# Three 1024 x 1024 x 1024 products of a hybrid encoder layer by Strassen's scheme, with weight operands made ahead and kept in DRAM

## The chip, the cores and the metric

The kernel runs on one core of one Trainium2 chip. The metric is the device time of one execution in microseconds (us); the times are the median and the extent of three runs. One further execution was taken by the hardware profiler, and all rows come from it.

## What is computed

One layer of a streaming encoder for 1024 tokens of width 1024, in f32. The change touches three products, `o @ W_attn_o`, `(gelu(gate) * hr) @ W_lru_o` and `mixed @ W_out`, each 1024 x 1024 by 1024 x 1024:

```python
h = rms_norm(x, norm_mix)
lru_in, lru_gate, q, k, v, g_lru, g_attn = split(h @ w_in)
hr = rg_lru(causal_depthwise_conv(lru_in, conv_w, conv_b), ...)
y_lru = (gelu(lru_gate) * hr) @ w_lru_o
y_attn = diff_attention(q, k, v, ...) @ w_attn_o
mixed = sigmoid(g_lru) * y_lru + sigmoid(g_attn) * y_attn
x = x + mixed @ w_out
x = x + memory_cross_attention(x, mem, ...)
x = x + hierarchical_moe(rms_norm(x, norm_ffn), ...)
```

## The kernel before

Every product is made of three matmuls per tile (`mm3`, L158): an f32 operand is split into a high part `h` (rounded to the engine's f32r by an ACT copy) and the remainder `l` (a DVE subtraction), and `wh*xh + wl*xh + wh*xl` is accumulated in PSUM. A matmul takes 128 x 128 stationary and 128 x 512 moving elements, so a 1024-cubed product has 8 x 2 x 8 x 3 = 384 of them.

All large tiles live in one pool `S` of 51 slots of 128 x 1024 f32. PSUM has four single banks (`bank`, 512 columns) and two double banks (`bank2`, 1024 columns). Weights come through the class `Weights`: a list of pieces of 512 KB in order of use, each loaded raw by SP's DMA queue (L78), copied to `wh` by ACT (L97) and subtracted to `wl` by DVE (L101). `W.tick` runs that stream ahead of the matmuls by up to `split_ahead` pieces; `W.take` hands over the next ones. The loads are tied to matmuls that went before. SP's queue has at most eight DMAs in flight, each waiting for the one eight places before it. Within an engine the instructions run in the order that the framework's scheduler gave them; the program's text, the waits and the slots that come free decide that order.

The stages, with their times in the trace: norm and start (0 to 40 us); q/k/v (to 304), where `tm_proj` (L331) makes 48 matmuls into a double bank for a quarter of a unit, ACT copies the bank out twice (`sq` L350 and `tm` L351), DVE and POOL apply norm and rotation, PE transposes (`pT`), ACT copies to `qk` (L375) and SP stores it to DRAM (L379); attention with the gate projections (to 711); the LRU, whose last chunks overlap the memory keys and values (to 910); then the three products. The attention output (L859 to L867, `pya`, 910 to 998) and the LRU output (L879 to L892, `pyr`, to 1085) loop over 8 blocks of output channels with the weight stationary (`cm_unit`); DVE multiplies the gate in and adds. w_out (L1209 to L1222, `pwo`, to 1175) has the mixed activation stationary, and adds x. After it the tokens are normalised (`st_A`), transposed (`phc`) and enter the cross attention (`pcq`, to 1358); 32 experts end the program (to 1946).

The lines that the prediction's steps touch:

```python
for j in range(2):                                  # tm_proj, L334
    for k in range(8):
        mm3(ps[:, j, :], hH[k][:, c], hL[k][:, c], wh, wl, k == 0, k == 7)
    W.tick(1)
...
def cm_unit(w, xh, xl, ps_halves):                  # 48 matmuls for a block of 128 output channels
```

Of the kernel before, what the change touches and what calls it, by code (L numbers as in the profile page):

```python
# [131 lines left out]
def block_kernel(ctx, tc, a):  # L132
# [198 lines left out]
    def tm_proj(w, qr, name):  # L331

        ps = bank2(name, F32, (P, 2, 512))
        for j in range(2):  # L334
            c = slice((2 * qr + j) * P, (2 * qr + j) * P + P)
            for k in range(8):
                wh, wl = (x[:, (k % 2) * 512:(k % 2) * 512 + 512] for x in w[k // 2])
                mm3(ps[:, j, :], hH[k][:, c], hL[k][:, c], wh, wl, k == 0, k == 7)
            W.tick(1)
        return ps  # L340

# [58 lines left out]

    W.split_ahead = 4
# [296 lines left out]
    zr, lru = [], {}  # L698
# [43 lines left out]
    def lru_scan(c):  # L742
# [23 lines left out]
        V.scalar_tensor_tensor(zr[c], zr[c], 0.5, q, op0=OP.mult, op1=OP.mult)  # L766
# [38 lines left out]
    def memory_values():  # L805
        w = W.take(4)
        vh, vl = slot("mvH", F32R, (P, 2, 512)), slot("mvL", F32R, (P, 2, 512))
# [11 lines left out]
    OS = 2  # L819
    oH, oL, oraw = [], [], []  # L820

    def o_split():
        for h in range(NH):
            oraw.append(slot(f"or{h}"))
            nc.sync.dma_start(oraw[h], oT_d[h])
            oH.append(slot(f"oH{h}", F32R))
            oL.append(slot(f"oL{h}", F32R))
            if OS == 1:
                split(oraw[h], oH[h], oL[h])
                oraw[h] = None  # L830
        for c in (slice(0, 512), slice(512, 1024)):
            for h in range(NH):
                if OS == 2:
                    split(oraw[h][:, c], oH[h][:, c], oL[h][:, c])
        oraw.clear()
# [4 lines left out]
    for op in LSEQ:  # L840
# [4 lines left out]
        elif op == "mv":  # L845
            mvH, mvL = memory_values()
        elif op == "mt":
            mkH, mkL = memory_keys_T(ktm)
        elif op == "o":
            o_split()  # L850
# [7 lines left out]
    ma = []  # L858
# [9 lines left out]
    del oH, oL  # L868


    zH, zL = [], []
    for c in range(8):
        zH.append(slot(f"zH{c}", F32R))
        zL.append(slot(f"zL{c}", F32R))
        split(zr[c], zH[c], zL[c])
    del zr
    mH, mL = [], []
    for j in range(8):
        w = W.take()[0]  # L879
        tr, m = slot(f"trb{j}"), ma[j]  # L880
        nc.sync.dma_start(tr, tg_d[8 + j])
        ps = bank2(f"pyr{j}")
        cm_unit(w, zH, zL, [ps[:, 0:512], ps[:, 512:]])
        V.scalar_tensor_tensor(tr, tr, 1.0, ps, op0=OP.add, op1=OP.mult)
        V.tensor_tensor(m, m, tr, op=OP.add)
        mH.append(slot(f"mH{j}", F32R))
        mL.append(slot(f"mL{j}", F32R))
        A.activation(mH[j], m, AF.Copy, scale=0.5)
        V.scalar_tensor_tensor(mL[j], m, 0.5, f(mH[j]), op0=OP.mult, op1=OP.subtract)
        W.tick()  # L890
        ma[j] = None
    del zH, zL, m  # L892
# [310 lines left out]
    x1 = []  # L1203
    for tb in range(NB):
        t = slot(f"x1_{tb}")
        nc.sync.dma_start(t, a["x"][tb * P:(tb + 1) * P, :])
        x1.append(t)
# [314 lines left out]
```

## Time and profile before

| | us |
|---|---|
| median of three runs | 1949.65 |
| lowest, highest | 1947.31, 1950.56 |
| the profiled execution | 1948.1 |
| its span in the trace | 1946.3 |
| PE busy | 1868.9 |
| DVE, ACT, POOL busy | 1296.6, 1103.5, 327.8 |
| attention output, LRU output, w_out | 88, 87, 90 |

The span is that of the core's instructions; the time around it is 1.8 us. A busy share of an engine is an average over stages of different kinds. What a stage can win is read in its own stretch of the trace, from the engine that is never idle there and from the waits that end last.

### The profile page before, as it was taken

What the parts mean: (1) busy time and instruction counts of PE and PEld (TensorE: products, weight loads), DVE (VectorE), ACT (ScalarE), POOL (GpSimd) and SP (SyncE); (2) the same over time, 40 slices, a digit from 0 to 9 for tenths busy, and PEclk for the clock granted to TensorE, in tenths of its full rate; (3) what the DMA queues carried; (4) which work ended last, traced back from release to release, by engine and by line L of the source; (5) the groups of instructions that cost most, each with busy time, mean ns of one, the idle gap of its engine ahead of it and who ended that gap; (6) DMA issues with size and microseconds to landing.
All of it is one profiled execution on the core that took longest, in us unless ns stands there. A gap on an engine that the chain in (4) does not pass through costs nothing. (4 is left out here: it accounts for less than half of the span.)

```text
span 1946.3 us, 25814 instructions
## 1 busy us (share of the span) xinstructions
PE 1868.9 (96%) x9214; PEld 1491.7 (77%) x9214; DVE 1296.6 (67%) x1766; ACT 1103.5 (57%) x1631; POOL 327.8 (17%) x432
## 2 busy tenths in 40 slices
PE   6999999999999999899999999996999999999996
PEld 5888888888888888778888887875777777777664
DVE  5222324677777758887444425675899999999985
ACT  5233324555555546876212215452888888888885
POOL 2144430122222221100000001111111111111110
PEclk9999999999999999999999999997999999999998
DMA  5222244433333121225322401177999999999996
GB/s 201 86 87 87 87 134 137 125 108 107 111 118 120 55 101 57 71 90 187 108 77 86 187 22 65 56 281 272 322 355 346 337 349 358 353 348 338 348 367 218
DMA packets 115027, 353.40 MB, mean 182 GB/s; under 512 B 14864, under 2 KB 28304, under 8 KB 114896
## 3 DMA queue, kind: packets, MB, share of 16 engines
q1 hardware_dynamic: 102992, 322.11, 46.9%
q0 software_dynamic: 7296, 17.04, 3.8%
q10 hardware_dynamic: 4608, 12.58, 1.6%
q8 instruction: 73, 1.20, 0.2%
q14 instruction: 58, 0.48, 0.1%
HBM read 311.82 MB, written 48.23 MB: 185 GB/s over the span
## 5 line engine op out<-in xcount | busy, mean ns | idle before, releaser
L101 DVE TENSOR_TENSOR wl<-wraw,wh 128x1024 fp32r<-128x1024 f32 x480 | 576.9, 1227 | 123.7 <-ACT wh L97 111.7
L97 ACT ACTIVATE wh<-wraw 128x1024 fp32r<-128x1024 f32 x480 | 496.3, 1057 | 113.0 <-PE pgu L161 15.9
L160 PE MATMUL pgu<-wl,xeh 128*96 128x512 f32 x512 | 203.7, 398 | 1.0 <-DVE wl L101 1.0
L159 PE MATMUL pgu<-wh,xeh 128*96 128x512 f32 x512 | 203.7, 398 | 0.3 <-ACT wh L97 0.3
L161 PE MATMUL pgu<-wh,xel 128*96 128x512 f32 x512 | 201.2, 393 | 0.0
L505 ACT ACTIVATE p<-pS,st 128x256 f32<-128x256 f32 (+7 forms) x128 | 94.9, 747 | 103.3 <-DVE st L498 51.7
L159 PE MATMUL pga<-hH,wh 128*128 128x512 f32 x320 | 127.4, 398 | 2.5 <-DVE wT L539 2.5
L160 PE MATMUL pga<-hL,wh 128*128 128x512 f32 x320 | 126.0, 394 | 0.0
L161 PE MATMUL pga<-hH,wl 128*128 128x512 f32 x320 | 125.5, 392 | 0.0
L160 PEld LDWEIGHTS pgu<-wl,xeh 128*96 128x96 f32 x512 | 82.9, 162 | 43.5 <-DVE wl L101 12.5
L159 PEld LDWEIGHTS pgu<-wh,xeh 128*96 128x96 f32 x512 | 83.0, 162 | 33.8 <-ACT wh L97 0.5
L161 PEld LDWEIGHTS pgu<-wh,xel 128*96 128x96 f32 x512 | 82.9, 162 | 33.4 <-DVE xel L329 0.2
L1351 POOL DMA_INDIRECT out<-y,idx x32 | 46.4, 1451 | 357.8 <-ACT y L1350 352.9
L514 POOL TENSOR_SCALAR p<-p,st 128x128 f32<-128x128 f32 (+3 forms) x64 | 55.0, 860 | 305.2 <-DVE st L513 159.4
L160 PE MATMUL py<-wl,ah 128*96 128x512 f32 x256 | 101.7, 397 | 0.3 <-DVE wl L101 0.2
L161 PE MATMUL py<-wh,ah 128*96 128x512 f32 x256 | 100.4, 392 | 0.0
L159 PE MATMUL pqk<-wh,hH 128*128 128x512 f32 x256 | 100.3, 392 | 0.0
L161 PE MATMUL pqk<-wh,hL 128*128 128x512 f32 x256 | 100.2, 391 | 0.0
L160 PE MATMUL pqk<-wl,hH 128*128 128x512 f32 x256 | 99.7, 389 | 0.0
L375 ACT ACTIVATE qk<-pT,gq 128x512 f32<-128x512 f32 x32 | 20.2, 686 | 106.8 <-PE pT L374 93.9
L159 PE MATMUL py<-wh,ah 128*96 128x512 f32 x256 | 80.0, 393 | 0.3 <-ACT wh L97 0.3
L493 PE MATMUL pS<-kH,qS 128*128 128x512 f32 (+2 forms) x192 | 69.5, 365 | 5.2 <-ACT p L505 5.2
(527 smaller groups left out, 4415.8 us busy)
## 6 DMA issues: line engine op xcount, KB each, us to landing
wraw<-in_w_gu SPq DMA_DIRECT2D x256, 512.0 KB
wraw<-in_w_dn SPq DMA_DIRECT2D x128, 512.0 KB
wraw<-in_w_cm SPq DMA_DIRECT2D x32, 512.0 KB
x<-in_x SPq DMA_DIRECT2D x16, 512.0 KB
wraw<-in_w_qk SPq DMA_DIRECT2D x32, 256.0 KB
qk_d<-qk SPq DMA_DIRECT2D x32, 256.0 KB
qr<-qk_d SPq DMA_DIRECT2D x32, 256.0 KB
kr<-qk_d SPq DMA_DIRECT2D x32, 256.0 KB
```

The lines of the kernel that those rows point to most:

```text
L97: ins = nc.scalar.activation(h, raw, AF.Copy)
L101: nc.vector.tensor_sub(l, raw, h.bitcast(F32))
L159: W.seen(E.matmul(out, lh, rh, start=start, stop=False))
L160: E.matmul(out, lh, rl, start=False, stop=False)
L161: E.matmul(out, ll, rh, start=False, stop=stop)
L375: A.activation(out[i][:, :, c], pt, AF.Copy, scale=gq[:, i:i + 1])
L493: E.matmul(ps[:, o:o + c], lhs, kh_[h, m][:, o:o + c], start=True, stop=False)
L505: A.activation(p[:, :n], ps[:, :n], AF.Exp, bias=mx[:, m:m + 1], accum_out=ls[:, m:m + 1])
L514: G.tensor_scalar(pp[1][:, :n], pp[1][:, :n], rl[:, 1:2], 0.0, op0=OP.mult, op1=OP.add)
L1351: G.indirect_dma_start(out=a["out"][:, :], out_offset=bass.IndirectOffsetOnAxis(ap=dest, axis=0), in_=y, in_offset=None, bounds_check=T - ...
```

## The change

Each of the three products is computed with seven products of half size (512 x 512 x 512, Winograd's form of Strassen's scheme): `multiply` runs, for each of the seven, four blocks of 128 output rows with four steps of 128 along the sum and `mm3`, 7 x 4 x 4 x 3 = 336 matmuls in place of 384. Seven operands on each side are sums of the four quarters of a matrix (`operand_steps`).

For the weights they are made during q/k/v: `prepare` loads the 24 quarters (512 KB each), forms the sums on DVE, splits each of the 42 operand tiles into `ph` and `pl` and stores both to DRAM (`pre_d`, 84 stores of 512 KB). `tm_proj` takes two steps of it at every tick (`PRE`). In the product they are loaded again (`preloaded`, 84 loads). For the activations `computed` makes them while the product before runs. Output sums run on DVE between the half-size products (`u1` to `u3`), and the gates are multiplied in by quarters (`gated`, `x1_add`). The 24 weight pieces leave the stream. The LRU's last step writes its result as quarters (`zq`), and o is loaded as quarters.

```diff
-    pieces += [a["w_ao"][j] for j in range(8)]
-    pieces += [a["w_lo"][j] for j in range(8)]
-    for hf in range(2):
-        pieces += [a["w_out"][hf, j] for j in range(4)]
...
             W.tick(1)
+            for _ in range(PRE[0]):
+                next(pre, None)
...
+    def operand_steps(q, moving, emit):
+        def lin(to, x, y, op):
+            for t, u, v in zip(q[to], q[x], q[y]):
+                V.tensor_tensor(t, u, v, op=op)
+        ADD, SUB = OP.add, OP.subtract
+        yield emit(0, q[0])
+        yield emit(1, q[2 if moving else 1])
+        for args in (((1, 3, 1, SUB), (0, 1, 0, ADD), (2, 2, 0, SUB)) if moving else
+                     ((2, 2, 3, ADD), (0, 2, 0, SUB), (1, 1, 0, SUB))):
+            yield lin(*args)
+        yield emit(2, q[0])
+        yield lin(0, 3, 0, SUB)
+        for n, i in ((3, 1), (4, 2), (5, 0), (6, 3)) if moving else ((3, 0), (4, 3), (5, 2), (6, 1)):
+            emit(n, q.pop(i))
+            yield
...
+            def emit(p, tiles):
+                h, l = slot(f"ph{n}{lp}{p}", F32R), slot(f"pl{n}{lp}{p}", F32R)
+                split(tiles[0], h, l)
+                nc.sync.dma_start(pre_d[n][p, lp, 0], f(h))
+                nc.sync.dma_start(pre_d[n][p, lp, 1], f(l))
+                if p == 5 and u + 1 < len(units):
+                    nxt.append(load(*units[u + 1]))
...
+    PRE[0] = 2
     for kind, i in order[1:len(order) - NL]:
         run(qk_steps(i) if kind == "qk" else v_steps(i))
+    run(pre)
...
+    def multiply(n, before, out):
+        lane = stages[n][2]
+        p1, u2, u3 = [None] * 2, [None] * 2, [None] * 2
+        for p in range(7):
+            g = 7 * n + p
+            ta, tb_ = ops.pop((g, 0)), ops.pop((g, 1))
+            for blk in range(4):
...
+                for k in range(4):
+                    rh, rl = (x[:, (k % 2) * 512:(k % 2) * 512 + 512] for x in tb_[k // 2])
+                    mm3(ps, *lane(ta, blk, k), rh, rl, k == 0, k == 3)
+                if blk == 0:
+                    if p < 6:
+                        before(p + 1)
+                    for d, kind in ((1, "computed"), (2, "preloaded")):
+                        for side in range(2):
+                            if (g + d) // 7 < len(stages) and stages[(g + d) // 7][side].__name__ == kind:
+                                operands(g + d, side)
...
+                if p == 0:
+                    A.activation(p1[lp][:, c], ps, AF.Copy)
+                elif p in (2, 3):
+                    to, x = (u2, p1) if p == 2 else (u3, u2)
+                    V.tensor_tensor(to[lp][:, c], x[lp][:, c], ps, op=OP.add)
+                else:
+                    out(p, blk, ps, {1: p1, 4: u3, 5: u3, 6: u2}[p][lp], c)
+                if p == 5:
+                    V.tensor_tensor(u2[lp][:, c], u2[lp][:, c], ps, op=OP.add)
...
-    for j in range(8):
-        w = W.take()[0]
-        t = slot(f"tga{j}")
-        nc.sync.dma_start(t, tg_d[j])
-        ps = bank2(f"pya{j}")
-        cm_unit(w, oH, oL, [ps[:, 0:512], ps[:, 512:]])
-        W.tick()
-        V.scalar_tensor_tensor(t, t, 1.0, ps, op0=OP.add, op1=OP.mult)
-        ma.append(t)
...
+    stages.append((preloaded("w_lo"), computed(zq, True), lane_out))
+    multiply(0, *gated(0, False))
+    stages.append((computed(mq, False, 0.5), preloaded("w_out"), lane_sum))
+    multiply(1, *gated(8, True))
...
+        if p == 5 and blk == 3:
+            W.split_ahead = 4
+            st_A(0)
+        if p == 6 and blk == 1:
+            st_A(1)
...
+    multiply(2, x1_load, x1_add)
```

Three places show how the order of the work changes. The first is SP's queue in q/k/v, from the stores of the second unit's first half (`qk_0`) to those of its second half (`qk_2`). Before, two weight pieces of 512 KB stood between them:

```order
L379 DMA qk_d_321<-qk_0_0_1067 128x512
L379 DMA qk_d_322<-qk_0_0_1067 128x512
L379 DMA qk_d_321<-qk_0_1_1068 128x512
L379 DMA qk_d_322<-qk_0_1_1068 128x512
L78 DMA wraw_1362<-in_w_qk 128x2x256 x2
L78 DMA wraw_1393<-in_w_qk 128x2x256 x2
L379 DMA qk_d_321<-qk_2_0_1239 128x512
```

In the changed kernel (its first twelve rows of 25; `phw_lo` and `plw_lo` are high and low part of an operand, `qw_lo` a quarter):

```order
L379 DMA qk_d_321<-qk_0_0_1160 128x512
L379 DMA qk_d_322<-qk_0_0_1160 128x512
L379 DMA qk_d_321<-qk_0_1_1161 128x512
L379 DMA qk_d_322<-qk_0_1_1161 128x512
L454 DMA pre_w_lo<-phw_lo_1412 128x1024
L455 DMA pre_w_lo<-plw_lo_1413 128x1024
L454 DMA pre_w_lo<-phw_lo_1443 128x1024
L454 DMA pre_w_lo<-phw_lo_1449 128x1024
L455 DMA pre_w_lo<-plw_lo_1444 128x1024
L455 DMA pre_w_lo<-plw_lo_1450 128x1024
L78 DMA wraw_1515<-in_w_qk 128x2x256 x2
L454 DMA pre_w_lo<-phw_lo_1518 128x1024
```

Between the two groups of `qk_d` stores now stand 14 operand stores, four quarter loads and the same two weight pieces.

The second is ACT in the same unit, from the copies of the first transposes (`qk_0`) to the copy of the second product out of PSUM (`sq_1`, `tm_1`). Before:

```order
L375 ACTIVATE qk_0_0_1067<-pT_0_0_1069,gq 128x2x256
L375 ACTIVATE qk_0_1_1068<-pT_0_1_1075,gq 128x2x256
L97 ACTIVATE wh_1106<-wraw_1018 128x1024
L97 ACTIVATE wh_1137<-wraw_1049 128x1024
L350 ACTIVATE sq_1_1145<-pqk_1_1081 128x1024
L351 ACTIVATE tm_1_1144<-pqk_1_1081 128x1024
```

In the changed kernel:

```order
L375 ACTIVATE qk_0_0_1160<-pT_0_0_1162,gq 128x2x256
L375 ACTIVATE qk_0_1_1161<-pT_0_1_1168,gq 128x2x256
L97 ACTIVATE wh_1199<-wraw_1097 128x1024
L324 ACTIVATE phw_ao_1206<-qw_ao_937 128x1024
L324 ACTIVATE phw_ao_1212<-qw_ao_935 128x1024
L97 ACTIVATE wh_1250<-wraw_1135 128x1024
L324 ACTIVATE phw_ao_1257<-qw_ao_933 128x1024
L324 ACTIVATE phw_lo_1263<-qw_lo_1218 128x1024
L350 ACTIVATE sq_1_1270<-pqk_1_1174 128x1024
L351 ACTIVATE tm_1_1269<-pqk_1_1174 128x1024
```

Four operand copies (`phw`) were put in between the weight copies and the two copies out of PSUM. In the fourth unit the same four stand there, in the first and the third unit one.

The third is DVE where the attention output begins: `op1` is an operand computed from the quarters of o (`oq`), `zq`, `r`, `i` and `q` belong to the last two LRU chunks. In the changed kernel:

```order
L921 TENSOR_TENSOR op100l<-oq_8148,op100h 128x1024
L921 TENSOR_TENSOR op101l<-oq_8150,op101h 128x1024
L411 TENSOR_TENSOR oq_8152<-oq_8160,oq_8152 128x1024
L826 SCALAR_TENSOR_TENSOR i_8189<-i_8189,xc_7979 128x1024
L836 SCALAR_TENSOR_TENSOR zq_8218<-gl_7821,q_8013 128x512
L836 SCALAR_TENSOR_TENSOR zq_8220<-gl_7821,q_8013 128x512
L411 TENSOR_TENSOR oq_8148<-oq_8152,oq_8148 128x1024
L411 TENSOR_TENSOR oq_8154<-oq_8162,oq_8154 128x1024
L824 SCALAR_TENSOR_TENSOR r_8188<-q_8211,r_8188 128x1024
L874 SCALAR_TENSOR_TENSOR mkL<-pmkT_8226,vec,mkH 128x512
L874 SCALAR_TENSOR_TENSOR mkL<-pmkT_8233,vec,mkH 128x512
L411 TENSOR_TENSOR oq_8150<-oq_8154,oq_8150 128x1024
```

Before, 16 subtractions `oL<-or,oH` of 512 columns stood here together, ahead of the last chunk's steps; now the operands' subtractions and sums alternate with them.

## Rows read from the trace of the kernel before

**Rows 1.** The page's head and part 1: busy time and share of each engine.

```profile
span 1946.3 us, 25814 instructions
...
PE 1868.9 (96%) x9214; PEld 1491.7 (77%) x9214; DVE 1296.6 (67%) x1766; ACT 1103.5 (57%) x1631; POOL 327.8 (17%) x432
```

**Rows 2.** Stretches (columns in the first line), the three rewritten stages.

```profile
core 0: us, PE busy (x) PEld busy (x) DVE busy (x) ACT busy (x) POOL busy (x), PEclk, DMA share, GB/s
...
910.00:998.00 88.00, 87.69 (x392) 72.33 (x391) 45.15 (x47) 32.79 (x41) 0.00 (x0) 1.00 0.31 103
998.00:1085.00 87.00, 87.00 (x385) 72.07 (x384) 34.88 (x29) 14.06 (x14) 0.61 (x4) 1.00 0.33 113
1085.00:1176.00 91.00, 90.84 (x413) 75.17 (x412) 33.14 (x40) 17.23 (x24) 2.97 (x8) 1.00 0.25 96
```

**Rows 3.** Waits of PE from 900 to 1190 us: total, times, longest.

```profile
PE pcqT L953 <- ACT cq L940: 0.7, 1, 0.7
PE pcq L159 <- DVE phc_0s L329: 0.3, 1, 0.3
PE pya L160 <- DVE oL L329: 0.3, 1, 0.3
PE pwo L159 <- DVE phc_0s L329: 0.2, 1, 0.2
```

**Rows 4.** Timeline of PE in w_out: start, duration.

```profile
1159.65 0.39 PE L160 MATMUL pwo<-wl,mH 128*128 128x512 f32 x1
1159.87 0.39 PE L161 MATMUL pwo<-wh,mL 128*128 128x512 f32 x1
...
1160.78 0.39 PE L159 MATMUL pwo<-wh,mH 128*128 128x512 f32 x1
```

**Rows 5.** Groups by line, 909 to 1176 us: busy us, mean ns, idle before.

```profile
L101 DVE TENSOR_TENSOR wl<-wraw,wh 128x1024 fp32r<-128x1024 f32 x25 | 30.3, 1219 | 1.8 <-ACT wh L97 1.2 <-PE pwo L160 0.5
L97 ACT ACTIVATE wh<-wraw 128x1024 fp32r<-128x1024 f32 x24 | 24.9, 1051 | 49.3 <-PE pwo L160 14.5 <-PE pya L161 10.5 <-DVE wl L101 10.4
...
L1217 DVE TENSOR_TENSOR x<-x,pwo 128x512 f32<-128x512 f32 x16 | 11.0, 687 | 46.5 <-PE pwo L161 46.5
```

**Rows 6.** Stretches: q/k/v, its stores, loads alone, experts (columns as Rows 2).

```profile
72.00:304.00 232.00, 232.00 (x1090) 193.46 (x1089) 66.91 (x55) 76.54 (x95) 92.59 (x96) 1.00 0.30 98
122.00:124.00 2.00, 2.00 (x11) 1.65 (x10) 0.31 (x1) 2.00 (x4) 0.00 (x0) 1.00 1.06 408
900.00:905.00 5.00, 5.00 (x24) 4.14 (x23) 5.00 (x5) 1.06 (x1) 0.00 (x0) 1.00 1.03 419
...
1392.00:1800.00 408.00, 408.00 (x1937) 288.00 (x1936) 374.95 (x380) 350.23 (x416) 56.78 (x46) 1.00 0.99 347
```

**Rows 7.** Timeline of the end of w_out.

```profile
1175.07 1.91 PE L920 MATMUL phc<-ident,tn 128*128 128x128 f32 x16
1177.29 0.50 PE L159 MATMUL pcq<-wh,phc_0s 128*128 128x512 f32 x1 [0.32 <-DVE phc_0s L329]
```

**Rows 8.** Timeline of SP in q/k/v: start, issue time of the group.

```profile
121.04 1.83 SPq L379 DMA_DIRECT2D qk_d<-qk  x4
...
138.22 1.82 SPq L379 DMA_DIRECT2D qk_d<-qk  x4
...
163.84 1.82 SPq L379 DMA_DIRECT2D qk_d<-qk  x4
...
186.97 1.82 SPq L379 DMA_DIRECT2D qk_d<-qk  x4
...
232.52 1.82 SPq L379 DMA_DIRECT2D qk_d<-qk  x4
...
258.14 1.80 SPq L379 DMA_DIRECT2D qk_d<-qk  x4
```

**Rows 9.** Timeline of ACT, second q/k unit.

```profile
148.73 1.03 ACT L351 ACTIVATE tm<-pqk 128x1024 f32<-128x1024 f32 x1
153.44 1.03 ACT L350 ACTIVATE sq<-pqk 128x1024 f32<-128x1024 f32 x1 [3.68 <-issue]
```

**Rows 10.** Groups by line, 72 to 304 us.

```profile
L97 ACT ACTIVATE wh<-wraw 128x1024 fp32r<-128x1024 f32 x18 | 18.1, 1069 | 0.0
```

More of the change, by code (lines that the diff above doesn't have):

```diff
@@ L765, in lru_scan @@
         yield
-        V.scalar_tensor_tensor(zr[c], zr[c], 0.5, q, op0=OP.mult, op1=OP.mult)
+        for hf in range(2):
+            i = 2 * (c // 4) + hf
+            if c % 2 == 0:
+                zq.setdefault(i, []).append(slot(f"zq{i}{c // 2 % 2}"))
+            tc_ = slice(TH[hf], TH[hf] + 512)
+            V.scalar_tensor_tensor(zq[i][-1][:, (c % 2) * 512:(c % 2) * 512 + 512], zr[c][:, tc_], 0.5, q[:, tc_],
+                                   op0=OP.mult, op1=OP.mult)
+        zr[c] = None
         yield
@@ L817, in memory_values, with half_T @@
         return vh, vl
[L819 to L835, printed above, removed]
+    def half_T(name, src, i, lp):
+        return quarter(name, src[4 * (i // 2) + 2 * lp:4 * (i // 2) + 2 * lp + 2, :, TH[i % 2]:TH[i % 2] + 512]
+                       .rearrange("h p c -> p h c"))
@@ new lines, in block_kernel, with preloaded @@
+    stages, ops = [], {}
+    QUARTER = {1: 0, 4: 2, 5: 3, 6: 1}
+    def preloaded(name):
+        while True:
+            for p in range(7):
+                r = []
+                for lp in range(2):
+                    t = [slot(f"{name}{p}{lp}{x}", F32R) for x in "hl"]
+                    for i in range(2):
+                        d = nc.sync.dma_start(f(t[i]), pre_d[name][p, lp, i])
+                        W.after(d, W.last)
+                    r.append(t)
+                yield r
@@ new lines, in computed, with emit @@
+    def computed(q, moving, scale=None):
+        done = []
+        def emit(p, tiles):
+            r = []
+            for lp, t in enumerate(tiles):
+                h, l = slot(f"op{len(ops)}{p}{lp}h", F32R), slot(f"op{len(ops)}{p}{lp}l", F32R)
+                if scale is None:
+                    W.after(A.activation(h, t, AF.Copy), W.last)
+                    V.tensor_tensor(l, t, f(h), op=OP.subtract)
+                else:
+                    W.after(A.activation(h, t, AF.Copy, scale=scale), W.last)
+                    V.scalar_tensor_tensor(l, t, scale, f(h), op0=OP.mult, op1=OP.subtract)
+                r.append((h, l))
+            done.append(r)
+        steps = operand_steps(q, moving, emit)
+        for _ in range(7):
+            while not done:
+                next(steps)
+            yield done.pop()
@@ L849, in block_kernel @@
         elif op == "o":
-            o_split()
+            oq = {i: [half_T(f"oq{i}{lp}", oT_d, i, lp) for lp in range(2)] for i in range(4)}
+            stages.append((preloaded("w_ao"), computed(oq, True), lane_out))
+            operands(0, 0)
+            operands(0, 1)
+            operands(1, 0)
         elif op == "s2":
@@ L876, in block_kernel @@
[L876 to L891, printed above, removed]
@@ L892, in block_kernel, with gated, before, out @@
-    del zH, zL, m
+    mq = {i: [None, None] for i in range(4)}
+    def gated(j0, add):
+        tg, tmp = {}, {}
+        def before(p):
+            if p in QUARTER:
+                i = QUARTER[p]
+                tg[i] = [half_T(f"tg{j0}_{i}{lp}", tg_d[j0:j0 + 8], i, lp) for lp in range(2)]
+        def out(p, blk, ps, prev, c):
+            i, lp = QUARTER[p], blk // 2
+            t = tg[i][lp]
+            if p in (1, 4) and lp not in tmp:
+                tmp[lp] = slot(f"y{j0}_{p}{lp}")
+            y = tmp[lp] if p in (1, 4) else prev
+            V.tensor_tensor(y[:, c], prev[:, c], ps, op=OP.add)
+            if blk % 2 == 1:
+                V.scalar_tensor_tensor(t, t, 1.0, y, op0=OP.add, op1=OP.mult)
+                m = mq[(0, 2, 1, 3)[i]]
+                if add:
+                    V.tensor_tensor(m[lp], m[lp], t, op=OP.add)
+                else:
+                    m[lp] = t
+                tg[i][lp] = None
+                tmp.pop(lp, None)
+        return before, out
```

100 lines of the change are left out of this document (73 added, 27 removed).

## The prediction, made before the change was run

> **What bounds the kernel now.** I read the page's first part first: TensorE is busy for 1868.9 of the 1946.3 us of the span, so a matmul taken away shortens the program unless something else takes its place [rows 1]. Then the table by stretches: in the three stages that the change rewrites (910 to 998, 998 to 1085, 1085 to 1176 us) PE is busy 87.69, 87.00 and 90.84 us of 88, 87 and 91 at a granted clock of 1.00, the higher of the two levels (2.4 GHz), while DVE is busy 33 to 45 us, ACT 14 to 33 and the DMA engines a quarter to a third [rows 2]. The list of waits says the same: from 900 to 1190 us PE waits 1.5 us in all [rows 3]. These stages are made of matmuls and nothing else. The reader should take one price from the timeline, the distance between two starts: 1159.65, 1159.87, ... 1160.78, five steps in 1.13 us, so 0.2265 us each [rows 4]. (The 0.39 us of a row is a modelled duration that overlaps the next one.) A check: 384 x 0.2265 = 87.0 us, the length of a stage.
>
> **What is removed.** Each 1024 x 1024 x 1024 product falls from 384 matmuls to 7 x 4 x 4 x 3 = 336 of the same form. 3 x 48 = 144 x 0.2265 = **-32.6 us**, all of it on the path.
>
> **What is added beside these matmuls.** Of the 24 weight pieces the splits go (24 ACT copies of 1.05 us, 24 DVE subtractions of 1.22 us) [rows 5]. In come, per product, 14 operand copies on ACT, 14 subtractions and 8 sums on DVE, and the output sums. With 1.22 us for 1024 columns and 0.69 for 512 [rows 5] DVE has about 54, 65 and 56 us of work in stages of 336 x 0.2265 = 76 us. It fits, and a half-size product (48 matmuls, 10.9 us) lies between the filling of a bank and its next use, so output sums have 10.9 us where they need up to 6. I cost them at nothing. If that cover is gone at a boundary, PE waits for the bank, a rival below. The reloads bring 44.0 MB in place of 12.6 MB. The stages now move some 103, 113 and 96 GB/s [rows 2], about 27.7 MB; 31.4 MB more in 233 us is 254 GB/s, against 419 GB/s in a stretch of nothing but loads [rows 6]. Nothing there either.
>
> **At two seams I count a loss.** The attention output starts with computed operands: eight quarter loads of o and four operand loads (6.3 MB, 15.4 us at the rate of the writes below) go out when the last readers of hH leave, then the subtractions and sums stand between the last scan's steps on DVE (the order above). By hand op110l ends about 1 us after PE wants it and op120l 0.3 us after: +1.5 us, bounds 0 and 6 (a late o quarter). At the end, the last two x blocks are complete only after the last half-size product, and the normalisation, the transposes and the first pcq follow at once. Before, pcq began 2.2 us after the transposes [rows 7]; by hand I get 3 us of idle PE against about 1: +2 us, bounds 0 and 4.
>
> **Where I see the real cost: q/k/v.** Here the change adds work to a stage in which PE is busy for 232.00 of 232 us, and adds DMA above all: 84 stores of 512 KB (44.0 MB) and 24 quarter loads (12.6 MB) on SP's one queue, beside 98 GB/s x 232 us = 22.7 MB at a busy share of 0.30 [rows 6]. A stretch that is mostly such stores ran at 408 GB/s with the engines full [rows 6], so the additions are 56.6 / 0.408 = 139 us of full DMA; with the 70 us already there, 209 of 232. Two steps per tick finish the 67 steps in 34 of 40 ticks, so the last 36 us get less and the earlier part is fuller still. I therefore count between the q/k stores, whose issue times stand in SP's timeline [rows 8]. SP keeps its order, so what stands between two of them must fit there:
> - 121.04 to 138.22 us: 8 stores, with the q/k and weight traffic 6.3 MB, 15.4 us in 17.2
> - 138.22 to 163.84: 10 stores and 4 quarters, 9.4 MB, 23.1 in 25.6
> - 163.84 to 186.97 (the order above): 14 stores and 4 quarters, 11.5 MB, **28.3 in 23.1**
> - 186.97 to 232.52: 16 stores and 4 quarters, 14.7 MB, 36.0 in 45.5
> - 232.52 to 258.14: 12 stores and 4 quarters, 10.5 MB, 25.7 in 25.6
>
> The third is over by 5.2 us. Who waits when DMA is late? Not only SP: the slots of the stored operands are reused, so ACT's copies of pqk out of PSUM wait until certain stores have landed, and PE has two double banks. In the second unit the copy of pqk1_1 ended at 148.73 + 1.03 = 149.76; the copy of the next product could start at 153.44, so PE took the freed bank at about 153.2: 3.4 us of slack [rows 9]. In the changed order four more ACT copies of 1.07 us [rows 10] stand ahead of it, 4.3 us, and its wait for the landing of two stores (2.6 us at 408 GB/s) comes on top: 1 to 3.5 us of idle PE, again in the fourth unit; in the first and the third only one copy is added, and they keep their slack. 5.2 + 2 x 2.3 = **+10 us**, bounds 0 (all of it slips into gaps) and 21 (the rate of the experts, rival 2). I take 10 because the rows nearest to stores, those of the q/k stores, ran at 408. The added ACT and DVE time itself (42 copies, 45 us; 42 subtractions and 24 sums, 81 us) fits beside the 76.54 and 66.91 us of the 232 there [rows 6].
>
> **Behind it.** Attention and LRU keep their work; 24 pieces fewer pass through the weight stream there. In the experts DMA is at 0.99 with 347 GB/s while PE is busy throughout [rows 6]; their loads are tied to PE's progress, so the stage starts earlier with its loads and keeps its length: nothing. If the loads were the limit there, they too would start earlier.
>
> **Sum**, on the profiled execution (1948.1 us): 1948.1 - 32.6 + 10 + 1.5 + 2 = 1929.0. The median shown is 1.55 us higher, so **1930.5 us** in its terms, its own range 1924 to 1938.
>
> **A rule against the change.** By this trace the engines carry 408 to 419 GB/s for short stretches and 347 at a share of 0.99 for 408 us [rows 6]. The Trainium skill, page "DMA: Bandwidth & Descriptors", section Specifications, gives a limit of about 358 GB/s of HBM per core. By that figure, as an estimate, the five windows would be over by some 14 us in place of 5.2, and the sum would be 1939. The short stretches speak against it as a hard limit; the 408 us are near it.
>
> **Rivals.**
> 1. *No stall in q/k/v.* Landings come before the copies need them. For it: between the groups of [rows 8] SP's queue holds only four weight loads each, so there is room to slip into. Then 1949.65 - 32.6 + 3.5 = **1920.5**. Chance 0.20.
> 2. *The sustained rate holds*: 347 / 0.99 = 350 GB/s, as in the experts. The five windows would then need 18.0, 26.9, 32.9, 42.0 and 30.0 us; four are over, by 0.8 + 1.3 + 9.8 + 4.4 = 16.3 us in place of 5.2. So 11 more is lost: **1941.5**. For it: 408 us of trace at that rate. Against it: that stretch has scattered transfers too, this one none. Chance 0.17.
> 3. *The queue locks PE to DMA* (the other side). A weight load for the next unit stands in SP's queue behind stores that wait for ACT; ACT waits to copy pqk until earlier stores have landed; PE waits for ACT. If every round of copy, store (eight in flight, 8 x 0.524 / 0.408 = 10.3 us), landing and copy costs more than a product and its transposes (12 us), each of the 16 products grows. It is slower from 29.1 / 16 = 1.8 us per product on; at 3 us, 48 us are lost: 1930.5 - 10 + 48 = **1968**. For it: the waits are in the order, and a full window leaves nothing to catch up with. Against it: most stores are waited for more than a product later. Chance 0.17.
> 4. *Product boundaries stall.* 21 boundaries of which each waits 1 us for operands or banks: 1930.5 + 21 = **1951**. For it: DVE is at 70 to 85% of these stages with PE in lockstep. Against it: 10.9 us of cover. Chance 0.09.
> The forecast keeps 0.37.
>
> **How the numbers follow.** 0.2% is 3.9 us, about what a measurement of this kernel can tell. Rivals 1 and 2 and the forecast are faster, 0.74 together; rival 4 is about the same, 0.09; rival 3 is slower, 0.17; with a little of the forecast's tail that is 0.73, 0.09 and 0.18. The range runs from below rival 1 (its two seams also at nothing: 1917, and 1 for the runs' spread) to 1955, beyond rival 4: left out is rival 3 with its long tail, and little else.
>
> **What would show it.** Right: 336 matmuls per stage and stages of 76 to 79 us; q/k/v 5 to 15 us longer, with PE's waits naming ACT's copies of pqk (their banks) or w_qk splits, and DMA near full between 121 and 260. Wrong: q/k/v unchanged (rival 1); PE waiting 40 us or more there (rival 3); PE waiting for DVE sums or for operands in the three stages (rival 4); an expert stage that grows by what was gained.

## The result and the profile after

The changed kernel takes 1967.72 us (median of four runs, 1963.25 to 1976.86), the kernel before on the same chip 1948.48. The ratio is 1.0105 with a 95% interval of 1.0065 to 1.0146: slower by about 19 us. The forecast of 1930.5 lay 19 us below the 1949.65 that the kernel before had on record. The profiled execution is the longest of the four, 1976.86 us with a span of 1975.0, so its stages carry some 9 us more than the median.

The first and last matmul of each stage (the views of single tiles: `pqk`, `pga`, the first operand of the attention output, `pcq`, `pgu`) give the length of every stage, to about 0.1 us; the attention ends with its last `pga`, where the LRU begins:

| stage, from first matmul to first matmul of the next | before | after | difference |
|---|---|---|---|
| q/k/v (from the first `pqk`) | 232.1 | 283.0 | **+50.9** |
| attention with gates | 406.1 | 405.8 | -0.3 |
| LRU | 199.4 | 204.3 | +4.9 |
| the three products, with the seam to `pcq` | 267.2 | 234.0 | **-33.2** |
| cross attention, routing | 181.1 | 177.8 | -3.3 |
| experts, to the end | 587.9 | 596.5 | +8.6 |

The head and the first part of the page of the changed kernel (busy time, share of the span and number of instructions of each engine):

```profile
span 1975.0 us, 26124 instructions
...
PE 1854.7 (94%) x9070; PEld 1470.1 (74%) x9070; DVE 1442.8 (73%) x1918; ACT 1145.0 (58%) x1667; POOL 354.5 (18%) x432
```

Its table by stretches, columns in the first line (PEclk is the granted clock, the share is that of the DMA engines):

```profile
core 0: us, PE busy (x) PEld busy (x) DVE busy (x) ACT busy (x) POOL busy (x), PEclk, DMA share, GB/s
72.00:357.00 285.00, 249.20 (x1098) 204.12 (x1097) 144.12 (x122) 118.57 (x139) 118.51 (x96) 0.93 0.76 279
...
950.00:1035.00 85.00, 84.56 (x377) 69.73 (x376) 69.14 (x70) 36.88 (x40) 1.20 (x1) 1.00 0.88 324
1035.00:1119.00 84.00, 84.00 (x372) 69.54 (x371) 61.23 (x58) 17.02 (x19) 0.61 (x4) 1.00 0.77 268
1119.00:1201.00 82.00, 80.62 (x372) 66.66 (x371) 63.10 (x80) 21.56 (x29) 5.63 (x8) 1.00 0.53 185
```

The lines from 950 to 1201 answer to [rows 2]: PE is as full as it was, DVE now 61 to 69 us per stretch, DMA 185 to 324 GB/s, and nothing holds PE up. The first line answers to the first of [rows 6]: PE is busy for 249.20 of 285 us at a granted clock of 0.93, where it was 232.00 of 232 at 1.00. DMA, at 0.76 of its time, is not full. The waits of PE in that stretch (total, times, longest):

```profile
PE pqk L159 <- ACT tm L351: 29.1, 6, 13.1
PE pv L159 <- ACT tm L351: 4.4, 1, 4.4
PE pT L374 <- POOL tm L364: 2.3, 2, 1.9
```

35.8 us of idle PE, nearly all of it named `ACT tm`, the copy of a product out of PSUM. The timeline around the longest wait (start, duration, engine, then the idle time before it) shows what stood ahead of that copy:

```profile
151.28 1.01 SPq L78 DMA_DIRECT2D wraw<-in_w_qk  x2
...
157.87 1.04 PE L374 MATMUL pT<-ident,tm 128*128 128x128 f32 x8
158.56 1.26 ACT L375 ACTIVATE qk<-pT,gq 128x512 f32<-128x512 f32 x2 [9.21 <-issue]
...
159.71 1.05 ACT L97 ACTIVATE wh<-wraw 128x1024 fp32r<-128x1024 f32 x1
...
160.66 2.00 ACT L324 ACTIVATE phw_ao<-qw_ao 128x1024 fp32r<-128x1024 f32 x2
...
161.74 1.28 SPq L454 DMA_DIRECT2D pre_w_ao<-phw_ao  x2
...
162.55 1.05 ACT L97 ACTIVATE wh<-wraw 128x1024 fp32r<-128x1024 f32 x1
...
163.50 1.05 ACT L324 ACTIVATE phw_ao<-qw_ao 128x1024 fp32r<-128x1024 f32 x1
163.57 0.96 SPq L431 DMA_DIRECT2D qw_lo<-in_w_lo  x1
...
165.88 3.47 SPq L431 DMA_DIRECT2D qw_lo<-in_w_lo  x3
...
170.41 1.06 ACT L324 ACTIVATE phw_lo<-qw_lo 128x1024 fp32r<-128x1024 f32 x1 [5.86 <-DMA qw_lo<-in_w_lo]
...
171.37 1.00 ACT L350 ACTIVATE sq<-pqk 128x1024 f32<-128x1024 f32 x1
...
172.27 1.01 ACT L351 ACTIVATE tm<-pqk 128x1024 f32<-128x1024 f32 x1
...
173.34 0.79 PE L159 MATMUL pqk<-wh,hH 128*128 128x512 f32 x1 [13.06 <-ACT tm L351]
```

ACT copies the transposes (158.56), then two weight tiles and three operand tiles (`wh`, `phw_ao`), then it wants the first quarter of the next weight: ACT stands idle for 5.86 us ahead of `phw_lo`. SP issued the first of those quarter loads only at 163.57: from 152.3 to 161.74 it had issued nothing, with the store of a `phw_ao` tile at the head of its queue that ACT had not yet made. Only then come `sq` and `tm` of the product that PE had finished long before, and PE, which needs that bank, restarts after 13.06 us. ACT is busy for 118.57 of the 285 us of this stage (42%); it is not short of time but in the wrong order.

The second loss is the clock. Three stretches from that restart on:

```profile
173.00:176.00 3.00, 2.66 (x6) 2.15 (x7) 2.58 (x3) 2.15 (x3) 1.98 (x2) 0.50 1.07 356
176.00:179.00 3.00, 3.00 (x8) 2.31 (x7) 3.00 (x4) 0.18 (x1) 2.83 (x3) 0.50 1.03 417
179.00:182.00 3.00, 3.00 (x14) 2.45 (x13) 2.59 (x3) 0.84 (x1) 3.00 (x2) 0.96 1.02 419
```

The granted clock is 0.50, the lower level (1.2 GHz), for about 6 us: in PE's timeline the starts are 0.43 us apart from 173.93 to 179.05, and 0.23 from then on. Starts 0.43 us apart follow five more waits, those of 4.00, 5.58, 1.90 (ahead of transposes), 3.10 and 4.40 us. So the 50.9 us of q/k/v are 35.8 us of waits and some 15 us more of busy PE (249.20 - 2 us of the stages beside it, against 232). Half speed explains nearly all of these: 72 starts of this stage lie 0.30 to 0.67 us apart in place of 0.23, in sum 13.8 us too far. The Trainium skill, page "TensorE: Matmul & The Clock Gate", Part 1, says that a PE which has stood idle is set back to half clock and has to work before it gets it back; the trace agrees (0.50 after 13.06 us of waiting). What comes behind a wait was in none of the forecast's terms.

### The profile page after: what moved, and what is told of

Same layout as the page of the kernel before. It is cut to its first block, busy times and chain, and to the rows that moved or that the text cites. A ratio compares the mean times of both kernels' runs of the same rounds, so it can differ in the third digit from the quotient of the medians.

```text
span 1975.0 us, 26124 instructions
## 1 busy us (share of the span) xinstructions
PE 1854.7 (94%) x9070; PEld 1470.1 (74%) x9070; DVE 1442.8 (73%) x1918; ACT 1145.0 (58%) x1667; POOL 354.5 (18%) x432
## 4 chain that ended last, share of the span: by engine, by line
PE 40%; issue 17%; DMA 15%; DVE 7%; ACT 4%; POOL 1%; POOLq 0%; ACTq 0%; SPq 0%; DVEq 0%
DMA out<-y,idx 13%; PE pw L159 4%; PE pw L160 4%; PE pw L161 4%; PE pga L159 3%; PE pga L160 3%; PE pga L161 3%; PE pS L557 1%; PE pS L558 1%; DVE st L562 1%; PE pw L599 1%; PE pcq L160 1%; PE pco L160 1%; PE pco L159 1%; PE pcq L161 1%
## 5 line engine op out<-in xcount | busy, mean ns | idle before, releaser
L101 DVE TENSOR_TENSOR wl<-wraw,wh 128x1024 fp32r<-128x1024 f32 x456 | 547.7, 1225 | 120.5 <-ACT wh L97 110.0
L97 ACT ACTIVATE wh<-wraw 128x1024 fp32r<-128x1024 f32 x456 | 472.4, 1057 | 78.7 <-DMA wraw<-in_w_dn 17.7
L159 PE MATMUL pqk<-wh,hH 128*128 128x512 f32 x256 | 105.1, 411 | 29.1 <-ACT tm L351 29.1
L161 PEld LDWEIGHTS pgu<-wh,xel 128*96 128x96 f32 x512 | 82.8, 162 | 33.2 <-DVE xel L325 0.2
L159 PEld LDWEIGHTS pqk<-wh,hH 128*128 128x128 f32 x256 | 50.4, 197 | 41.6 <-ACT tm L351 31.3
```

The costliest lines, as they stand in the source:

```text
L97: ins = nc.scalar.activation(h, raw, AF.Copy)
L101: nc.vector.tensor_sub(l, raw, h.bitcast(F32))
L159: W.seen(E.matmul(out, lh, rh, start=start, stop=False))
L161: E.matmul(out, ll, rh, start=False, stop=stop)
```

## The experiments

The length of q/k/v (from the first `pqk` to the first `pga`; 232.1 before) is the measure beside the time, since the other stages hardly move, but for the attention, which has a column too, and the experts, which vary from run to run. All edits are short diffs against the changed kernel. Of the three theories at the start A and B put the loss on the stores, by the waits in SP's queue (rival 3) or by their bytes (rival 2); C puts it on the work added to ACT and DVE in the chain that ends with the copies out of PSUM.

| run | time, us | ratio to before (95%) | q/k/v | attention |
|---|---|---|---|---|
| the change | 1967.72 | 1.0105 (1.0065 to 1.0146) | 283.0 | 405.8 |
| e1 products only | 1931.46 | 0.9906 (0.9879 to 0.9934) | 240.2 | 405.9 |
| e2 few stores | 1955.63 | 1.0038 (1.0026 to 1.0051) | 269.4 | 405.7 |
| e3 early loads | 1966.19 | 1.0093 (1.0062 to 1.0124) | 279.8 | 405.9 |
| e4 stores from POOL | 1974.67 | 1.0130 (1.0105 to 1.0155) | 292.5 | 405.7 |
| e5 evict first | 1940.89 | 0.9945 (0.9924 to 0.9966) | 252.4 | 406.4 |
| e6 evict first, few stores | 1929.95 | 0.9894 (0.9869 to 0.9919) | 245.5 | 405.8 |
| e7 evict first, early loads | 1938.17 | 0.9938 (0.9919 to 0.9957) | 249.7 | 405.7 |
| e8 spread into the attention | 1951.78 | 1.0017 (0.9998 to 1.0036) | 232.0 | 437.4 |
| e9 three steps | 1947.83 | 0.9995 (0.9980 to 1.0010) | 246.2 | 417.2 |
| e10 half pace, old order | 1975.24 (one run) | | 243.4 | 445.7 |
| e11 no sums | 1929.07 (one run) | | 237.1 | 406.1 |
| e12 uneven steps | 1952.92 | 1.0013 (0.9998 to 1.0028) | 238.8 | 430.6 |
| e13 two products | 1940.19 | 0.9947 (0.9924 to 0.9970) | 235.9 | 410.5 |

**e1: the products alone.** One operand pair per weight is made, and every reload reads it.

```diff
+        for n in pre_d:
+            t = quarter(f"q{n}", a[n][0, 0] if n == "w_out" else half(a[n], 0, 0))
+            h, l = slot(f"ph{n}", F32R), slot(f"pl{n}", F32R)
+            split(t, h, l)
+            nc.sync.dma_start(pre_d[n][0, 0, 0], f(h))
+            nc.sync.dma_start(pre_d[n][0, 0, 1], f(l))
+            yield
...
-                        d = nc.sync.dma_start(f(t[i]), pre_d[name][p, lp, i])
+                        d = nc.sync.dma_start(f(t[i]), pre_d[name][0, 0, i])
```

> Leaves out the making of the weight operands: one operand tile pair per weight is made and stored (3 loads, 6 stores), and every reload reads that pair, so the values of the three products are not the reference's. The products, their 84 reloads and all their sums stay. All theories of the loss in q/k/v expect the stage at its old length and the products' gain whole: 1948.5 - 33 + 3, that is 1916 to 1922 us. If part of the loss came from the products or from what follows them, it is above 1927.

1931.46 us: the gain of the products is there (234.0 us from first operand to `pcq`, as in the change), but q/k/v still lost 8.1 us, with three loads and three copies. ACT's timeline shows how little it takes:

```profile
84.70 1.04 ACT L97 ACTIVATE wh<-wraw 128x1024 fp32r<-128x1024 f32 x1
93.51 1.06 ACT L324 ACTIVATE phw_out<-qw_out 128x1024 fp32r<-128x1024 f32 x1 [7.76 <-DMA qw_out<-in_w_out]
94.47 1.00 ACT L350 ACTIVATE sq<-pqk 128x1024 f32<-128x1024 f32 x1
...
108.10 1.26 ACT L375 ACTIVATE qk<-pT,gq 128x512 f32<-128x512 f32 x2 [11.70 <-PE pT L374]
...
112.05 1.03 ACT L351 ACTIVATE tm<-pqk 128x1024 f32<-128x1024 f32 x1
```

One operand copy waits 7.76 us for its quarter, the copies out of PSUM stand behind it (`sq` starts at 94.47, before the change at 83.61), the transposes come late (11.70 us of idle ACT ahead of `qk`), and at 113.13 PE has waited 4.64 us for the `tm` of 112.05. The stated 1916 to 1922 was missed by this and by 7 us in the experts of the profiled run, a stage that varied between 585.6 and 596.5 us over all these kernels without a pattern that we found; the eight distances between the scatters of its last experts but one, 152 us in sum in place of 145, make the difference.

**e2: six stores in place of 84.**

```diff
-                nc.sync.dma_start(pre_d[n][p, lp, 0], f(h))
-                nc.sync.dma_start(pre_d[n][p, lp, 1], f(l))
+                if p == 0 and lp == 0:
+                    nc.sync.dma_start(pre_d[n][p, lp, 0], f(h))
+                    nc.sync.dma_start(pre_d[n][p, lp, 1], f(l))
```

(and the reload of e1)

> Keeps every load, copy, subtraction and sum of the preparation, but stores only one pair per weight (6 stores in place of 84) and reloads that pair, so the products' values are not the reference's. Theory A (order: ACT's operand copies wait for quarter loads that stand in SP's queue behind stores, and the copies out of PSUM stand behind them) and theory B (bytes: q/k/v has no DMA time for 44 MB of stores) both expect 1918 to 1928 us. Theory C (the added ACT and DVE work itself delays the copies out of PSUM) expects 1955 us or more.

q/k/v keeps 37.3 of its 50.9 us of loss. Theories A and B fall as main causes: with 6 stores left of 84 the loss is still three quarters of what it was, and DMA is busy for 0.42 of the stage. The timeline before one of the waits has no DMA wait in it:

```profile
157.16 1.03 PE L374 MATMUL pT<-ident,tm 128*128 128x128 f32 x8
157.85 1.26 ACT L375 ACTIVATE qk<-pT,gq 128x512 f32<-128x512 f32 x2 [8.77 <-PE pT L374]
...
159.01 1.06 ACT L97 ACTIVATE wh<-wraw 128x1024 fp32r<-128x1024 f32 x1
...
159.96 2.00 ACT L324 ACTIVATE phw_ao<-qw_ao 128x1024 fp32r<-128x1024 f32 x2
...
161.85 1.05 ACT L97 ACTIVATE wh<-wraw 128x1024 fp32r<-128x1024 f32 x1
162.80 1.05 ACT L324 ACTIVATE phw_ao<-qw_ao 128x1024 fp32r<-128x1024 f32 x1
...
163.74 1.05 ACT L324 ACTIVATE phw_lo<-qw_lo 128x1024 fp32r<-128x1024 f32 x1
...
164.69 1.01 ACT L350 ACTIVATE sq<-pqk 128x1024 f32<-128x1024 f32 x1
...
165.59 1.02 ACT L351 ACTIVATE tm<-pqk 128x1024 f32<-128x1024 f32 x1
...
166.67 0.79 PE L159 MATMUL pqk<-wh,hH 128*128 128x512 f32 x1 [6.65 <-ACT tm L351]
```

From 159.01 on ACT copies without a gap, four operand tiles and two weight tiles, and then `sq` and `tm`; PE has waited 6.65 us for them. That is theory C in one sharper form (called C' from here): the order.

**e3: quarter loads early, and e4: stores from POOL's queue.**

```diff
-                if p == 5 and u + 1 < len(units):
+                if p == 2 and u + 1 < len(units):
```

```diff
-                nc.sync.dma_start(pre_d[n][p, lp, 0], f(h))
-                nc.sync.dma_start(pre_d[n][p, lp, 1], f(l))
+                nc.gpsimd.dma_start(pre_d[n][p, lp, 0], f(h))
+                nc.gpsimd.dma_start(pre_d[n][p, lp, 1], f(l))
```

> The four quarter loads of the next unit are issued with the third operand instead of the sixth; same bytes, same instructions. Theory A expects most of the 52 us of q/k/v back: 1930 to 1942 us, with ACT's waits for quarter loads gone. Theory B expects no change: 1960 to 1975 us, PE waiting as long for other landings.

> The 84 stores are issued from POOL's queue instead of SP's; same bytes, so that loads no longer stand behind stores that wait for ACT and DVE. Theory A expects 1930 to 1945 us. Theory B expects 1960 us or more. A cost of its own could be POOL's time for 84 issues, which delays the rotation of q and k: then PE waits for POOL's tm.

e3 gains 3.2 us of q/k/v, e4 loses 9.5. The late load at 163.57 in the timeline above was real, but one wait of many: SP's queue order is not the main cause. (e4 also takes POOL's time for the issues, so it tells less than e3.) Both times lie where theory B had them; what speaks against B as the main cause is e2.

**e5: the copies out of PSUM first.** The preparation's steps leave the product loop and follow the copies:

```diff
             W.tick(1)
-            for _ in range(PRE[0]):
-                next(pre, None)
...
             A.activation(tm, ps, AF.Copy)
+            for _ in range(2 * PRE[0]):
+                next(pre, None)
```

(and the same ahead of the `yield` of `v_steps`)

> The two preparation steps of every tick are taken out of the product loop and issued, four at a time, after the two copies of the bank out of PSUM; same work, same bytes. So on ACT only the two weight copies stand between the copies of the first transposes and the second copy out of PSUM, as before the change. Theory C' (the operand copies ahead of the copies out of PSUM in ACT's order make PE wait, and PE's clock falls after each wait) expects most of the 39 us back that the run with few stores lost in q/k/v, hence 1925 to 1940 us if the stores themselves cost 10 us or less. Theory B (bytes) expects at least the 13 us between the change and the run with few stores to stay and waits on landings to show: 1940 to 1955 us. If neither order nor stores matter (DVE or POOL is late), 1960 us or more, with PE waiting for POOL's tm.

1940.89 us, 27 us below the change, by two moved lines and two more in the v units. q/k/v falls from 283.0 to 252.4 us, and PE's waits there from 35.8 to 13.0:

```profile
PE pqk L159 <- ACT tm L349: 9.5, 5, 2.8
PE pv L159 <- ACT tm L349: 1.9, 1, 1.9
PE pT L374 <- POOL tm L364: 1.6, 2, 1.1
```

The longest is now 2.8 us. Work, bytes and number of instructions are those of the change; the order alone moved 30.6 us of q/k/v. The edit moves the steps on ACT, DVE and SP together. That ACT's place is the one that counts is read from the waits and the timelines (`ACT tm` ended nearly all of PE's waits, and in e2 nothing but copies stood ahead of it); no run moved ACT's copies alone. The median is just above the range of C' and inside that of B, so the time by itself does not choose between them, and e6 had to.

**e6 and e7: what is left with the better order.** e6 is e5 with the six stores of e2, e7 is e5 with the early loads of e3.

> The edit of e5 and 6 stores in place of 84 (the reloads read one pair, the products' values are not the reference's). Theory C' expects q/k/v near its old length plus at most 8 us: 1920 to 1930 us. The difference to e5 is what the stores cost with the better order: 0 to 5 us by C', 10 us or more by B. If DVE or POOL is the late one, 1945 us or more.

> The edit of e5, and the quarter loads issued with the third operand as in e3. Theory A (late quarter loads hold up ACT) expects 8 us or more below e5; C' alone expects within 5 us of e5.

The stores cost 252.4 - 245.5 = 6.9 us of q/k/v with this order and 283.0 - 269.4 = 13.6 with the change's. By the medians e6 is 10.9 us below e5. C' had 0 to 5 us for the stores and B 10 or more, so the stores have a part of their own beside the order. The early loads bring 2.7 us, as C' had it. In e5 the DMA engines are at 0.87 to 0.95 of their time between 122 and 322 us and move 327 to 354 GB/s. Whether the stores cost by their bytes or by the waits that hang on them is not shown.

**e8: half the pace, the rest in the attention.** Two steps per product in place of four, at e5's place, and the last 27 in the gate projections. (e8, e9, e10, e12 and e13 also have e3's early loads.)

```diff
+            for _ in range(PRE[0]):
+                next(pre, None)
...
-    run(pre)
...
             W.tick()
+            next(pre, None)
             A.activation(t[:, c], ps, fn, scale=scale)
```

> The preparation at half the pace (two steps after each copy out of PSUM in place of four) and its last 27 steps during the gate projections between the attention's parts, one per half projection; the quarter loads early. Same work and bytes in all. Both C' and B expect the q/k/v stage to come near its old length (plus 0 to 10 us); the attention has PE busy for 398 of 407 us with DVE at 71%, so up to 10 us may be lost there: 1922 to 1940 us. If DVE's added work is what delays q/k/v, half the loss stays: 1945 us or more.

q/k/v is back at 232.0 us, to the tenth. So there is a slack, and two steps per product stay within it. But the 27 steps that went into the attention cost it 31.3 us, more than one microsecond each: PE's waits from 300 to 760 us are 29.6 us in place of 7.7, half of them for the softmax's `p` from ACT. The expectation had 0 to 10 us there, and the stated 1922 to 1940 was missed by it; the total is no better than before.

**e9, e10, e11.** e9 has three steps per product at e5's place, from the third product of the first v unit on; e10 has e8's pace in the change's order; e11 is e6 without the 24 sums on DVE.

> The order of e5 (steps after the copies out of PSUM, quarter loads early) at three steps per product in place of four, begun two products earlier, so that all of it still ends with q/k/v and the attention is left alone. The stage cost +20 us at four steps and 0 at two (e8). If the loss grows with the load beyond a threshold (theory: slack used up), three steps cost 3 to 10 us: 1920 to 1932 us. If it follows the number of steps made in q/k/v (theory: each step costs its share), 66 of 67 steps cost the 17 us of e7 again: 1936 to 1942 us.

> The pace of e8 (half in q/k/v, the rest in the gate projections) with the order of the change: the steps stand in the product loop, ahead of the copies out of PSUM. e8 had q/k/v at its old 232 us. If the order decides by itself, q/k/v is 10 us or more above 232; if only the load decides, it is within 4 us of 232. The attention is expected to lose about 31 us as in e8.

> e6 (better order, 6 stores) without the 24 sums on DVE in the preparation (the products' values are not the reference's). e6 left q/k/v 13 us longer than before. If DVE's added time is what remains (it delays the norm, POOL's rotation and with it the transposes), q/k/v falls from 245.5 to 232 to 238 us. If it is ACT's 42 copies or the late quarter loads, it stays at 243 or more.

e10's 243.4 against e8's 232.0 (one profile each) shows the order again, at half the load: 11 us. (Its attention lost 39.6 us where 31 were expected; why is open.) e11, in one run, shows 8.4 us of DVE's sums. They stand between the norm's steps on DVE, and POOL, which rotates q and k in the same chain, is slowed beside them. Groups by line on POOL in this stage (behind the count the busy time in us and the mean ns of one), first of the kernel before, then of e6:

```profile
L364 POOL TENSOR_TENSOR tm<-tm,sq 128x256 f32<-128x256 f32 x16 | 12.8, 797 | 1.1
...
L361 POOL TENSOR_TENSOR sq<-tm,ropeS 128x128 f32<-128x128 f32 x16 | 7.3, 458 | 16.6 <-DVE tm L356 16.6
```

```profile
L364 POOL TENSOR_TENSOR tm<-tm,sq 128x256 f32<-128x256 f32 x16 | 18.9, 1180 | 1.3
...
L361 POOL TENSOR_TENSOR sq<-tm,ropeS 128x128 f32<-128x128 f32 x16 | 16.6, 1038 | 22.5 <-DVE tm L356 16.4 <-ACT tm L349 4.7 <-issue 1.4
```

The 128 x 128 step `L361` took 458 ns and takes 1038, the 128 x 256 step `L364` 797 and 1180; in e11, without the sums but with the subtractions, 824 and 1019. (In the change itself `L361` took 778 ns and `L364` 793.) These means mix two lengths. Two steps of e6 with the DVE instruction beside each, in the timeline:

```profile
115.96 0.45 POOL L361 TENSOR_TENSOR sq<-tm,ropeS 128x128 f32<-128x128 f32 x1
116.03 1.47 DVE L356 TENSOR_TENSOR tm<-tm,rq_2r 128x1024 f32<-128x1024 f32 x1 [0.51 <-POOL rq_2r L225]
...
161.91 1.22 DVE L325 TENSOR_TENSOR plw_ao<-qw_ao,phw_ao 128x1024 fp32r<-128x1024 f32 x1
162.17 1.28 POOL L361 TENSOR_TENSOR sq<-tm,ropeS 128x128 f32<-128x128 f32 x1 [1.43 <-DVE tm L356]
```

Of the 16 steps `L361` of e6, 11 started while a DVE instruction with two inputs in SBUF was running and took 1278 to 1322 ns; the other 5 took 448 to 457. Before the change none started so, and all took 453 to 465. The Trainium skill, page "SBUF — State Buffer", section "Who interferes with whom", says that a DVE instruction with two inputs in SBUF contends with a GpSimd instruction that reads SBUF; the sums and subtractions here are of that kind, and the rows agree. e11's own 237.1 leaves 5 us for the copies, the subtractions and the loads.

e9 missed both stated ranges of time: q/k/v +14.1 and the attention +11.1. PE waited 4.8 us for `qS`, the first heads' operand, which e12 shows more clearly.

**e12: steps where there is room.** Two and three in turn in q and k, five per product in the last v unit.

> A candidate: the order of e5 with the steps where the engines have room: four per product in the last two products of the first v unit, two and three in turn in q and k, five in the last v unit, which has no norm and no rotation; all 67 end with q/k/v. If the slack theory holds, q/k/v loses 0 to 6 us and the program takes 1916 to 1926 us; if each step costs its share, 1936 us or more.

q/k/v +6.7, but the attention +24.5, and the stated 1916 to 1926 was missed. PE's waits from 300 to 760 us, then SP's queue ahead of the longest (start, time in the queue, line, transfer):

```profile
PE pS L560 <- DVE qS L535: 16.9, 2, 13.4
PE pS L560 <- ACT p L572: 8.0, 10, 2.9
```

```profile
324.22 0.32 SPq L457 DMA_DIRECT2D pre_w_out<-plw_out  x1
325.53 0.32 SPq L456 DMA_DIRECT2D pre_w_out<-phw_out  x1
326.18 0.52 SPq L524 DMA_DIRECT2D qr<-qk_d  x1
326.83 0.49 SPq L457 DMA_DIRECT2D pre_w_out<-plw_out  x1
...
337.13 0.44 SPq L525 DMA_DIRECT2D qr<-qk_d  x1
```

`qS` is made from the loads `qr`. The stores of the last steps fill SP's queue up to 326.83. The first `qr` goes out at 326.18, 14 us after the first `pga` (before the change at 285.54, 19 us ahead of it), the last of these at 337.13, and the first attention matmul waits 13.4 us in one piece. So the burst of stores at the end of this stage is paid for by the next; that is read from the trace, no run moved these stores alone.

**e13: two of three products.** w_out goes back to 384 matmuls; 45 steps, two per product (three in the last two products of the first v unit), in e5's order.

```diff
-    pre_d = {n: dp.tile([7, 2, 2, P, 1024], F32, name=f"pre_{n}") for n in ("w_ao", "w_lo", "w_out")}
+    pre_d = {n: dp.tile([7, 2, 2, P, 1024], F32, name=f"pre_{n}") for n in ("w_ao", "w_lo")}
...
-    multiply(2, x1_load, x1_add)
+    for hf in range(2):
+        w = W.take(4)
...
+                mm3(ps, sH[:, c], sL[:, c], w[k // 2][0][:, kc], w[k // 2][1][:, kc], k == 0, k == 7)
```

> w_out goes back to the 384 matmuls of the kernel before; the attention output and the LRU output stay with seven half-size products. Their preparation is 45 steps: three per product in the last two products of the first v unit, two per product after, in the order of e5, so that nothing is left for the attention. By e8, q/k/v at two steps per product costs nothing, and here no head load waits behind stores at its end. Theory (the loss is load beyond the slack of ACT's and DVE's chain): q/k/v 232 to 236 us, attention 406 to 408, the products 267 - 22 = 245, so 1948.5 - 22 + 4 - 2 + 2, that is 1926 to 1934 us. If instead every step costs its share wherever it lies (theory of shares: 45 of 67 of the 17 to 20 us of e5 and e7, 12 us), 1938 us or more.

The stages came as the slack theory had them (steps cost nothing until the slack of the chain is used up), a little above: q/k/v +3.8, attention +4.4, the products 244.8 (-22.4). By shares q/k/v would have lost 12 us. The median of 1940.19 is nevertheless above the stated 1926 to 1934, since LRU, attention and q/k/v together cost 13 us of the 22; by the time alone the theory of shares (1938 or more) would have fitted. Two products with little loss are worth what three with more loss are. Of the kernels that compute the whole reference e7, e5 and e13 are the fastest, 0.5 to 0.6% below the kernel before; their intervals overlap.

## Why the prediction was wrong, point by point

- *The matmuls removed, -32.6 us*: right. The three products take 234.0 us in place of 267.2, -33.2, the same within 0.2 us in every run that has all three.
- *Sums, operands and reloads beside the matmuls at nothing*: right. PE waits 1.7 us in all between 966 and 1202 us, for `phc`, `pmkT` and `pcq`. Rival 4 (product boundaries) did not happen.
- *The two seams, +1.5 and +2*: the LRU before the first product grew by 4.9 us in the change (3.9 to 5.1 in the others), the end of w_out is within the -33.2, and the cross attention became 3.3 us shorter. In sum +1.6 for +3.5. No wait of PE names an operand of the first product. What lengthens the LRU was not taken apart; PE's waits in it are 2.8 us longer, 2.0 of them for `mem`, and the rest stays open. So the sum came near for reasons that the two terms do not hold.
- *q/k/v, +10 us with bounds 0 and 21*: **this is the step that failed; it measured +50.9.** It was sized by DMA time between the q/k stores. The windows were over by 5.2 us on paper (the group of q/k stores at 215.31 was left out of them, so the fourth window is two). But DMA was at 0.76 of its time in the stage, and taking 78 of the 84 stores out gave back 13.6 us of the 50.9 (e2), so bytes were not the main loss. A stretch as full as 176 to 182 us, mostly stores, moved 417 to 419 GB/s, above the 350 GB/s of the experts (rival 2). The Trainium skill, page "DMA: Bandwidth & Descriptors", section Specifications, has about 358 GB/s of HBM per core, and this stretch lies above that too. No long stretch of the change's q/k/v was full, so a limit over a long time was not tested. The second half of the term, ACT's order, had the right place (the copies `phw` ahead of `sq` and `tm`) and far too small a price: 2 x 2.3 us. Three things were missing in it. What an operand copy itself waits for (a quarter load, a DVE sum) was not charged to the copies behind it, although ACT runs its instructions in order: 5.86 us in the longest wait. The slack of 3.4 us [rows 9] was taken as if the chain ahead of it (norm, POOL's rotation, transposes, copy) kept its length, while DVE's work stands in it and POOL's first step took 778 ns in place of 458. And the waits of 3.10 us and more bring 3 to 6 us at half clock behind them, of which half is lost.
- *The added ACT and DVE time fits*: true as a sum (ACT 118.57 and DVE 144.12 us of 285) and useless: an engine that is 42% busy held PE up for 33.5 us.
- *Rival 3*, the slower side, gave 1968 and the time came out at 1967.72, at a chance of 0.17. Its chain (a load behind stores that wait for ACT, ACT behind the load, PE behind ACT) is what the longest wait shows, but its price was for stores in flight; with six stores in place of 84, 37.3 of the 50.9 us stay (e2). So the time agrees by luck, by the 3 us per product that were chosen for it, and not by the mechanism.
- *Rival 1* (no stall) holds for two steps per product in the better order (e8: 232.0).
- *Nothing behind it*: attention right; the experts were 8.6 us longer in the profiled run of the change and 0.7 in e3. The stage lies between 585.6 and 596.5 us over all the kernels, so this looks like its spread, and like the part of the profiled execution above the median; no run took it apart.

In numbers: of the 50.9 us, 30.6 go with the order (e5), 6.9 of the rest with the stores (e6), 8.4 with DVE's sums (e11, one run), and 5.0 are left, which no run took apart. These shares, of one profile each, are taken off in this sequence; in another (stores first, e2: 13.6) they come out otherwise, since the waits of one kind hide those of another.

## What to carry to other kernels

Background work on an engine that also frees PSUM banks is priced by its place in that engine's order, not by the engine's busy share: issue it behind the copies that the matmuls wait for, and let nothing that waits for a load or another engine stand ahead of them. Find the slack of that copy in the trace (here 3.4 us), and put no more work per product ahead of or within its chain than fits. Count the matmuls at half clock behind the waits too (here behind those of 3.10 us and more), and look at which loads of the next stage a burst of stores will delay.

## What the runs showed of the hardware

- After waits of 3.10, 4.00, 4.40, 5.58 and 13.06 us PE ran at half clock for 3 to 6 us, 6 us of it behind the longest as behind the shortest of these, 3 us behind two between; after 1.36 and 2.01 us (at 213.05 and 258.06) the starts were 0.23 to 0.24 us apart behind a first of 0.34, while 1.90 us ahead of transposes was followed by a slow stretch of about 1 us of matmuls.
- One core moved 417 to 419 GB/s over two stretches of 3 us that were mostly stores, the same as with loads alone [rows 6].
- POOL's 128 x 128 rotation step `L361` took 448 to 457 ns in e6, but 1278 to 1322 when it started while DVE ran an instruction with two inputs in SBUF. The profile names no wait for it, only a longer instruction, and the mean (1038 ns) hides the two lengths.
- The same 84 stores issued from POOL's queue made q/k/v 9.5 us longer than from SP's (292.5 against 283.0, one profile each).
